# Where the first chunk's u in float32 comes from: kept from its making, or summed from its hi and lo

## The chip, the core and the metric

The kernel runs on one core of a Trainium2 chip, in one launch. The metric is the device time of one execution in microseconds (us). The core has five engines that run their own queues of instructions in the order in which they were put there and wait for one another by semaphores: PE (TensorE, products and transposes), DVE (VectorE), ACT (ScalarE), POOL (GpSimd) and SP (SyncE, which here only issues DMAs; POOL issues some too).

## The reference

What is computed is two layers of a diffusion backbone on 512 latent tokens and 256 context tokens of width 1024. Each layer is a half-step SwiGLU, a token mixer and a second half-step SwiGLU; the mixer of the first layer is an RG-LRU beside windowed attention, that of the second is dense attention. Each of the six sub-layers has the form below.

```python
def _rmsnorm(x, g):
    return x * lax.rsqrt(jnp.mean(x * x, axis=-1, keepdims=True) + EPS) * g

def _modulate(h, shift, scale):
    return h * (1 + scale) + shift

def _ffn_sublayer(h, shift, scale, gate, g_pre, g_post, w_gate, w_up, w_down):
    u = _modulate(_rmsnorm(h, g_pre), shift, scale)
    y = (jax.nn.silu(u @ w_gate) * (u @ w_up)) @ w_down
    return h + FFN_RES * gate * _rmsnorm(y, g_post)
```

## The kernel before

All six sub-layers run on one core, one after the other. Products are made in float32 from float32r passes: an operand is split exactly into hi (its 12 leading bits, a cast on ACT) and lo (the rest, a subtraction on DVE; both are issued by `halves`, L193, or by `hilo`, L724 and L725), and hi\*hi, hi\*lo and lo\*hi are summed. The 768 tokens are six tiles of 128, in two chunks of three tiles (512 tokens in two chunks of two tiles in the last two sub-layers, where the context is no longer wanted).

**The end of a sub-layer.** Its last product is token-major and is made by `type2`, once for each chunk: the down projection of a SwiGLU (names such as `d010a` and `d011a`: layer 0, second SwiGLU, chunk 0 and chunk 1) or the out-projection of a mixer (`eo0a`, `eo1a` of the first layer's, `oo0a`, `oo1a` of the second's). `type2` steps over k-tiles of 128 rows of the weights. For each it loads and splits the weights (`d011w`, 1024 columns as two halves) and makes the left operand: `hr` is a load of 128x384, `hh` its hi and lo; in the out-projections `oh` and `ooh` are made from tiles that lie in SBUF. With three token tiles a k-tile takes 18 matmuls of 512 columns (three tiles, two halves, three passes), with two token tiles 12. The last four k-tiles (`STAG`) are taken tile by tile, and each token tile then goes to `finish`.

**The boundary.** `boundary` squares and weighs the sum y of a token tile (L505, L506) and returns `rest`, which loads the residual x (L512, on POOL's queue), updates it (L514, DVE), stores it (L518) and calls `make_u`. `make_u` normalises x (the square with its sum on ACT, L410; the scaling on POOL, L414), transposes it in eight blocks on PE (`b_0utp`, L419), applies shift and scale (four blocks on ACT, L395; four on DVE, L393) into `ut`, a tile of float32 from the two slots of the tag `bu`, and splits `ut` into hi and lo, columns of the next u (L193, `u_0h`, `u_0l`).

**Where it stands.** For the tiles of the first chunk, `rest` is not run at once: it is put on the list `later`, and the `type2` of the second chunk takes one entry from `later` at each odd k, before the weights and the left operand of that k. The boundary of the first chunk's three tiles thus lies beside the second chunk's products.

**The sums.** A SwiGLU takes its features from the third on by seven block products instead of eight, for which sums of blocks of u are wanted, T1 to T4. An object of the class `Sums` makes them ahead of three sub-layers: the second SwiGLU of layer 0 and both SwiGLUs of layer 1. It needs the first chunk's u in float32. `Sums.prepare` makes it anew: hi plus lo, in six or four tiles of 128x512, two for each token tile, by POOL (L437), 16 instructions in all. `prepare` is the last entry of `later`. The three places are the second chunks of the products ahead of them, `eo1`, `d011` and `oo1`; the SwiGLU at the very start has a class of its own (`FirstSums`).

**Slots and order.** The tiles of `prepare` come from the tag `c3`, which has 23 slots of 3 KB a partition; `hr`, `hh`, `oh` and `ooh` take slots of the same tag. A scheduler places the instructions on the engines by a model of when each could run, and what is placed decides the order on the chip; slots of a tag are handed out in the order in which the program asks for them, so a tile is not begun before the tiles asked for ahead of it on its tag have their slots.

Of the kernel before, what the change touches and what calls it, by code (L numbers as in the profile page):

```python
"""Two-layer diffusion backbone (SwiGLU halves around an RG-LRU / windowed-attention mixer and a
dense-attention mixer) on one core.

float32 products run as float32r passes: an operand is split exactly into hi (its 12 leading bits)
and lo (the rest), and hi*hi + hi*lo + lo*hi is accumulated in float32.
"""
# [6 lines left out]
F32 = mybir.dt.float32  # L13
# [4 lines left out]
P = 128  # L18
# [10 lines left out]
class Net:  # L29
# [5 lines left out]
    # ---------------------------------------------------------------- set-up  # L35
# [17 lines left out]
    def psum_phase(self, all=False):  # L53
        """Six banks, or all, change hands: what follows waits bank by bank for what came before."""
        while len(self.pools) > (0 if all else 1):
            self.pools.pop().__exit__(None, None, None)
        self.nph = getattr(self, "nph", 0) + 1
        self.accs = 4 if all else 3
        self.pp = self.psum_pool(f"psum{self.nph}")
# [17 lines left out]
    def c3(self, shape, dt, name):  # L77
        """A tile of at most 3 KB a partition, from the slots that h and the mixers share."""
        return self.sb.tile(shape, dt, tag="c3", bufs=23, name=name)

    def late(self, ins):
        """A load that keeps its place behind what was issued before it on its queue."""
        return self.tc.keep_in_program_order(ins)
# [7 lines left out]
    # ------------------------------------------------- adaLN modulation, blocks 2p and 2p+1 of 18  # L91
    def tick(self, n=1):
        """n steps of the work that runs beside the rest."""
# [10 lines left out]
    def ada_steps(self, p):  # L104
        nc, cp = self.nc, self.cp
        acc = self.adatile(f"ada{p}")
        for k in range(KD):
            raws = []
            for b in range(2):
                l, j = divmod(2 * p + b, 9)  # L110
                src, name = self.a["w_ada"][l, k * P:(k + 1) * P, j * D:(j + 1) * D], f"wa{p}_{k}{b}"
                if p > 2:
                    # room where nothing else is now
# [57 lines left out]
    # ------------------------------------------------------------- weights  # L171
# [5 lines left out]
    def weights(self, src, name):  # L177
        """A [128, n] block of weights as hi and lo, 512 columns at a time."""
# [12 lines left out]
    def halves(self, hi, lo, src, eng=None, late=False):  # L191
        """src = hi + lo, exactly."""
# [11 lines left out]
    # ------------------------------------------------------------ residual stream and u  # L204
# [14 lines left out]
    # ------------------------------------------------- the first sub-layer's lead  # L219
    def opening(self, u, w, products):  # L220
        """The first modulation comes by halves of D, the second half's weights behind all else that the first half's
        products take: three of the four products of the first features start on the first half of D."""
# [3 lines left out]
        def ada_load(h, k):  # L226
            """Columns of half h of shift and scale."""
# [47 lines left out]
        def ada(h, ks=range(KD)):  # L275
            """The sums over even and odd tiles of D apart, so that four products run at a time."""
# [42 lines left out]
        def modulate(c, h):  # L319
            """zt -> u in float32, in place, and its hi and lo."""  # L320
# [54 lines left out]
    def make_u(self, x, z, t, i_shift, u, c, j, sums, name):  # L375
        """x [128 tokens, D] in SBUF -> columns 128j.. of u[c] (hi and lo of [128, KD, tokens]); z: room for x
        normalised. sums: also what the seven products of the next sub-layer take from u."""
# [7 lines left out]
        ut = bp.tile([P, KD, P], F32, tag="bu", bufs=2, name=name + "ut")  # L385
        ut = [ut[:, 0:4], ut[:, 4:8]]
# [11 lines left out]
        if sums is not None:  # L398
            # the tile before: what the next products wait for goes first
            sums.catch_up()  # L400
            if c == 1:
                sums.due = (j, ut, z)
# [19 lines left out]
    class Sums:  # L422
        """T1 = B12 - B11, T2 = B22 - T1, T3 = B12 - B22, T4 = B21 - T2, where u is [[B11, B12], [B21, B22]]:
        halves of D by chunks of tokens."""
# [4 lines left out]

        def prepare(self):  # L430
            """The first chunk once more in float32."""
            nc = self.net.nc
            for j in range(self.n // P):
                self.first[j] = [self.net.c3([P, 4, P], F32, f"b{h}{j}_{self.nm}") for h in range(2)]
                for h in range(2):
                    hi, lo = (x[:, 4 * h:4 * h + 4, j * P:(j + 1) * P].bitcast(F32) for x in self.u[0])
                    nc.gpsimd.tensor_add(self.first[j][h], hi, lo)  # L437
# [6 lines left out]
        def add(self, j, ut, z):  # L444
            """The columns of token tile j of the second chunk."""
# [10 lines left out]
        def most(self):  # L456
            """hi and lo of T1, T2 and T3."""
# [8 lines left out]
        def last(self):  # L466
            """T4 takes the place of B12."""
# [3 lines left out]
    class FirstSums:  # L471
        """The same from the first sub-layer's u in float32, in pairs of tiles of D."""
# [21 lines left out]
    def boundary(self, t, y, g, xsrc, xdst, nxt, name):  # L494
        """x += G * rms(y) for the tokens of tile t; then the next sub-layer's u. Frees y; the rest is returned."""
# [6 lines left out]
        for i in range(2):  # L502
            # a bank of y each
# [19 lines left out]
    # ------------------------------------------------------------ SwiGLU  # L523
# [3 lines left out]
    def ffn(self, l, s, u, sums, tiles, gate, finish, hook=None, joint=False):  # L527
        """tiles: the token tiles of the two chunks; finish(chunk, j, acc, G) takes the products."""
# [7 lines left out]
        def products(f, c, ks=range(KD)):  # L536
# [8 lines left out]
            # tiles of D first where they come one by one  # L545
# [13 lines left out]
        else:  # L559
            w[0] = self.ffn_weights(l, s, 0)  # L560
            self.rest()
            # the first features: the first chunk leads, since the second chunk's u comes late
# [10 lines left out]
        # as many tokens at a time as there are banks for  # L573
# [14 lines left out]
    def strassen(self, l, s, u, sums, n, hd, joint):  # L588
        """The features from the third on, two tiles at a time, by seven products (Strassen's, in Winograd's form):
        A = W^T in blocks of (feature tile) x (half of D), B = u in blocks of (half of D) x (chunk of tokens)."""  # L590
# [15 lines left out]
        def job(p, b, h):  # L606
# [5 lines left out]
            # the sums take the places of their terms  # L612
# [6 lines left out]
            # the banks that the features before hold longest come last  # L619
# [45 lines left out]
    def type2(self, nm, nk, lhs, nt, wsrc, finish, n=D, hook=None):  # L665
        """Token-major products: nt tiles of [128 tokens, n]; wsrc(k) is the rows of k-tile k."""
# [15 lines left out]
        for j in range(nt):  # L682
            # the very last tile by halves, so that what follows starts early
# [5 lines left out]
    def rest(self):  # L689
        """What the second chunk's tiles of the sub-layer before have left to do."""  # L690
# [13 lines left out]
    def type1(self, nm, src, nf, u, finish):  # L704
        """Feature-major products: nf tiles of [128 features, 2 chunks of tokens]; src(f) is the weights of tile f."""
# [22 lines left out]
    # ------------------------------------------------------------ RG-LRU || windowed attention  # L728
# [18 lines left out]
    def even(self, u, gate_i, finish):  # L747
# [3 lines left out]
        # recurrent branch: projection and convolution  # L751
# [88 lines left out]
        # gate of the recurrent branch  # L840
# [17 lines left out]
        # queries, keys, values  # L858
# [4 lines left out]
        def roped(src, t, name):  # L863
            """src [128 tokens, 10 heads * 64] in PSUM -> SBUF, rotated for the tokens of x."""
# [51 lines left out]
        def gelu():  # L916
            # once the tables of the recurrence are done with
# [8 lines left out]
        def qkv_early(t, acc):  # L926
            # the scores of the first tile start before the last queries are ready
# [19 lines left out]
        # attention  # L947
# [12 lines left out]
    def softplus8(self, src):  # L960
        """-8 softplus(-lam) and 8 softplus(-lam), [128, 8]."""
# [7 lines left out]
        # log1p(e) = 2 artanh(e / (2 + e))  # L969
# [15 lines left out]
    def pt(self, tp):  # L985
        """hi and lo of a block of transposed probabilities, in one of three places."""
# [436 lines left out]
```

## Time and profile before

| | |
|---|---|
| median of 3 runs | 2635.53 us |
| the three runs | 2635.57, 2626.84, 2635.53 us |
| span of the profiled execution | 2636.3 us |
| PE busy | 2546.2 us, 97% of the span |
| DVE busy | 1757.5 us, 67% |
| ACT busy | 1351.8 us, 51% |
| POOL busy | 325.3 us, 12% |

The span is that of one execution taken with the profiler; it is 0.8 us above the median of the runs. PE's share is near the whole span, but its idle time is not spread evenly: it lies at the start and at the boundaries between sub-layers, and there the chain of small steps on ACT, DVE and POOL is what a reader has to follow. PEclk in a row is the clock that TensorE was granted, 1.00 for 2.4 GHz and 0.50 for 1.2 GHz.

### The profile page before, as it was taken

The page shows a single profiled execution, that of the slowest core. Times are in us where ns is not written, and L with a number is a line of the kernel's source. Part 1 is how long each engine was busy: PE and PEld are TensorE (multiplying, and loading weights), DVE is VectorE, ACT ScalarE, POOL GpSimd, SP SyncE. Part 2 cuts the span into 40 slices and gives each one's busy share as a digit, 9 for nine tenths or more (in the row PEclk, how much of TensorE's full clock was granted, in tenths as well). Part 3 has the DMA queues.
Part 4 walks back from the last instruction along what each step waited for, and adds up shares of the span by engine and source line. Part 5 has one row for each costly group of instructions (what it writes and reads, how often), then busy time and mean ns, then how long its engine had stood idle before and what let it go on. Part 6 is the DMA issues. An engine that isn't in the chain of part 4 may idle for free.

```text
span 2636.3 us, 38740 instructions
## 1 busy us (share of the span) xinstructions
PE 2546.2 (97%) x13980; PEld 2237.5 (85%) x13980; DVE 1757.5 (67%) x3199; ACT 1351.8 (51%) x2783; POOL 325.3 (12%) x356
## 2 busy tenths in 40 slices
PE   7999999999999999999999999999999899899998
PEld 5899998889855789999888899998887667799986
DVE  5766664658777686767555767665557657899843
ACT  4444444547566654444454544444545556666632
POOL 4000000213022240000011300000122221400000
PEclk8999999999999999999999999999999999999999
DMA  7445436541387443232555332235554552544542
GB/s 275 144 160 168 152 127 206 192 160 53 119 293 266 157 141 96 96 105 100 187 184 189 124 97 95 98 107 177 198 181 152 200 176 82 177 135 128 161 167 88
DMA packets 147761, 403.00 MB, mean 153 GB/s; under 512 B 16504, under 2 KB 33576, under 8 KB 147568
## 3 DMA queue, kind: packets, MB, share of 16 engines
q1 hardware_dynamic: 136688, 362.00, 41.6%
q0 software_dynamic: 10880, 38.53, 4.2%
q8 instruction: 109, 1.79, 0.3%
q14 instruction: 84, 0.69, 0.1%
HBM read 351.91 MB, written 48.55 MB: 152 GB/s over the span
## 4 chain that ended last, share of the span: by engine, by line
PE 80%; DVE 7%; issue 5%; ACT 3%; POOL 3%; DMA 2%; POOLq 0%; DVEq 0%; ACTq 0%; SPq 0%
PE px L601 17%; PE py L601 12%; PE pz L601 12%; PE d110a L701 4%; PE d100a L701 4%; PE d000a L701 4%; PE d010a L701 4%; PE ada L122 3%; PE d001a L701 3%; PE d101a L701 3%; PE eo0a L701 1%; PE oq1a L701 1%; PE qkv1a L701 1%; PE opT L1286 1%; PE gu L201 1%
## 5 line engine op out<-in xcount | busy, mean ns | idle before, releaser
L210 POOL TENSOR_TENSOR b_0pr<-b_0pv,mhalf 128x1 f32<-128x1 f32 x4 | 2.2, 560 | 983.9 <-DVE b_0pv L208 983.9
L634 DVE TENSOR_TENSOR cp<-px,cp 128x384 f32<-128x384 f32 (+1 forms) x160 | 76.5, 520 | 56.3 <-PE px L601 56.3
L724 ACT ACTIVATE hh<-hr 128x384 fp32r<-128x384 f32 x132 | 68.6, 521 | 81.5 <-DMA hr<-hd 80.6
L725 DVE TENSOR_TENSOR hh<-hr,hh 128x384 fp32r<-128x384 f32 x132 | 72.9, 559 | 50.6 <-ACT hh L724 49.5
L636 ACT ACTIVATE h<-cp 128x384 f32<-128x384 f32 (+1 forms) x160 | 77.0, 498 | 26.1 <-DVE cp L634 21.9
L122 PE MATMUL ada<-wa,sc 128*32 128x512 f32 x512 | 83.8, 611 | 0.5 <-DVE cols L137 0.4
L634 DVE TENSOR_TENSOR cp<-pz,cp 128x384 f32<-128x384 f32 (+1 forms) x80 | 41.9, 524 | 57.4 <-PE pz L601 56.4
L638 DVE TENSOR_TENSOR h<-cp,h 128x384 f32<-128x384 f32 (+1 forms) x160 | 79.6, 519 | 0.4
L629 ACT ACTIVATE cp<-px 128x384 f32<-128x384 f32 (+1 forms) x160 | 71.4, 446 | 0.0
L634 DVE TENSOR_TENSOR cp<-py,cp 128x384 f32<-128x384 f32 (+1 forms) x80 | 41.7, 521 | 26.7 <-PE py L601 17.2
L614 DVE TENSOR_TENSOR w<-w,w 128x512 f32<-128x512 f32 x80 | 56.8, 709 | 1.6 <-DMA w<-in_wgu_dram 0.2
L193 DVE TENSOR_TENSOR d110w_0lo<-d110w,d110w_0hi 128x512 fp32r<-128x512 f32 x22 | 15.2, 691 | 63.6 <-ACT d110w_0hi L193 63.6
L617 DVE TENSOR_TENSOR w<-w,w 128x512 f32<-128x512 f32 x80 | 55.3, 691 | 2.0
L615 DVE TENSOR_TENSOR w<-w 128x512 f32<-128x512 f32 x80 | 55.2, 690 | 1.9
L616 DVE TENSOR_TENSOR w<-w,w 128x512 f32<-128x512 f32 x80 | 55.1, 689 | 1.5
L701 PE MATMUL d011a<-d011w_0hi,hh 128*128 128x512 f32 x132 | 52.7, 399 | 0.2 <-ACT hh L724 0.2
L701 PE MATMUL d101a<-d101w_0hi,hh 128*128 128x512 f32 x132 | 52.5, 398 | 0.0
L701 PE MATMUL d001a<-d001w_0hi,hh 128*128 128x512 f32 x132 | 52.5, 398 | 0.0
L701 PE MATMUL d100a<-d100w_512hi,hh 128*128 128x512 f32 x132 | 52.4, 397 | 0.0
L701 PE MATMUL d000a<-d000w_512hi,hh 128*128 128x512 f32 x132 | 52.4, 397 | 0.0
L701 PE MATMUL d010a<-d010w_0hi,hh 128*128 128x512 f32 x132 | 52.3, 396 | 0.0
L701 PE MATMUL d101a<-d101w_512hi,hh 128*128 128x512 f32 x132 | 52.2, 396 | 0.0
(5579 smaller groups left out, 9579.9 us busy)
## 6 DMA issues: line engine op xcount, KB each, us to landing
w<-in_wgu_dram SPq DMA_DIRECT2D x175, 512.0 KB, 3.5
wa<-in_w_ada_dram SPq DMA_DIRECT2D x204, 256.0 KB, 4.6
hd<-h SPq DMA_DIRECT2D x66, 384.0 KB, 4.7
hr<-hd SPq DMA_DIRECT2D x132, 192.0 KB, 3.7
wa<-in_w_ada_dram SPq DMA_DIRECT2D x42, 512.0 KB, 4.3
d000w<-in_w_down_dram SPq DMA_DIRECT2D x22, 512.0 KB, 3.5
d001w<-in_w_down_dram SPq DMA_DIRECT2D x22, 512.0 KB, 3.8
d010w<-in_w_down_dram SPq DMA_DIRECT2D x22, 512.0 KB, 3.9
```

What stands on the lines that cost most here:

```text
L122: ins = nc.tensor.matmul(acc[32 * g:32 * g + 32, :], lhsT=self.sc[:, k, :], rhs=raws[g], start=(k == 0), stop=(k == KD - 1), skip_group_ch ...
L601: mm = lambda x, y, **kw: nc.tensor.matmul(out, lhsT=x, rhs=y, skip_group_check=True, **kw)
L614: nc.vector.tensor_sub(x3, x1, x3)
L615: nc.vector.tensor_add(x1, x1, x2)
L617: nc.vector.tensor_sub(x4, x4, x2)
L629: nc.scalar.activation(t, src, AF.Copy)
L634: nc.vector.tensor_add(t, acc, t)
L636: nc.scalar.activation(hc, t, AF.Silu)
L638: nc.vector.tensor_mul(hc, t, hc)
L701: mm(acc[:, h:min(h + 512, n)], lhsT=x[xi][:, js], rhs=w[h // 512][wi], start=(k == 0 and xi == 0 and wi == 0), stop=(k == nk - 1 and xi = ...
L724: self.nc.scalar.activation(t[:, 0], src, AF.Copy)
L725: self.nc.vector.tensor_sub(t[:, 1], src, t[:, 0].bitcast(F32))
```

## The change

In `make_u`, where the tile belongs to the first chunk and the next sub-layer has a `Sums`, the float32 u is no longer written into the shared tile of the tag `bu`. It goes into two tiles of 128x512 of the tag `c3`, which are entered in `sums.first` and stay there until the sums have used them. `prepare`, its 16 additions on POOL and its entry in `later` are gone. The tiles of `c3` are now asked for in `make_u`, that is at k = 1, 3 and 5 of the second chunk (1 and 3 in `oo1`), ahead of the left operand of that k. Comments are left out of the file too, so line numbers move: L701 becomes L696, L724 and L725 become L719 and L720, L395 and L393 become L399 and L397, L410 and L414 become L414 and L418, L419 becomes L423, L505 becomes L500, L514 becomes L509.

```diff
@@ make_u
-        ut = bp.tile([P, KD, P], F32, tag="bu", bufs=2, name=name + "ut")
-        ut = [ut[:, 0:4], ut[:, 4:8]]
+        if sums is not None and c == 0:
+
+            ut = sums.first[j] = [self.c3([P, 4, P], F32, f"{name}b{h}") for h in range(2)]
+        else:
+            ut = bp.tile([P, KD, P], F32, tag="bu", bufs=2, name=name + "ut")
+            ut = [ut[:, 0:4], ut[:, 4:8]]
...
@@ class Sums
-        def prepare(self):
-            """The first chunk once more in float32."""
-            nc = self.net.nc
-            for j in range(self.n // P):
-                self.first[j] = [self.net.c3([P, 4, P], F32, f"b{h}{j}_{self.nm}") for h in range(2)]
-                for h in range(2):
-                    hi, lo = (x[:, 4 * h:4 * h + 4, j * P:(j + 1) * P].bitcast(F32) for x in self.u[0])
-                    nc.gpsimd.tensor_add(self.first[j][h], hi, lo)
...
@@ body
-                if sn is not None and (c, j) == (0, len(tl[s][0]) - 1):
-                    self.later.append(sn.prepare)
```

The order of the instructions on the engines moves at the three places. In the names below `hh_1` is the left operand of k-tile 1 of `d011`, and so on; `x4` after a row stands for four instructions alike.

PE in `d011` before, where the transposes of the first token tile stand:

```order
L701 MATMUL d011a_13188<-d011w_0hi,hh_1_13269 128x512
L701 MATMUL d011a_13188<-d011w_512hi,hh_1_13269 128x512
L419 MATMUL b_0utp_13235<-ident,b_0y 128x128 x4
L419 MATMUL b_0utp_13246<-ident,b_0y 128x128 x4
L701 MATMUL d011a_13189<-d011w_0hi,hh_1_13269 128x512
L701 MATMUL d011a_13189<-d011w_512hi,hh_1_13269 128x512
```

PE in `d011` after, from the last matmuls of k-tile 0:

```order
L696 MATMUL d011a_13180<-d011w_0hi,hh_0_13193 128x512
L696 MATMUL d011a_13180<-d011w_512hi,hh_0_13193 128x512
L423 MATMUL b_0utp_13227<-ident,b_0y 128x128 x4
L423 MATMUL b_0utp_13238<-ident,b_0y 128x128 x4
L423 MATMUL b_1utp_13328<-ident,b_1y 128x128 x4
L423 MATMUL b_1utp_13339<-ident,b_1y 128x128 x4
L696 MATMUL d011a_13178<-d011w_0hi,hh_1_13261 128x512
```

Before, the 18 matmuls of k-tile 0 and 12 of k-tile 1 stand ahead of the transposes; after, k-tile 0 alone does, and the second tile's transposes follow at once.

ACT before, at the end of `d010`, ahead of the first square of the boundary:

```order
L193 ACTIVATE d010w_512hi<-d010w_13049 128x512
L724 ACTIVATE hh_5_13469<-hr_5_13467 128x384
L193 ACTIVATE d010w_0hi<-d010w_13064 128x512
L193 ACTIVATE d010w_512hi<-d010w_13064 128x512
L724 ACTIVATE hh_6_13502<-hr_6_13500 128x384
L505 ACTIVATE b_0q,b_0s<-d010a_12422 128x512 x2
```

ACT after, in `d011`, from the first tile's shift and scale:

```order
L399 ACTIVATE b_0ub_13225<-b_0utp_13227,cols_7779,gs_8146 128x128 x4
L193 ACTIVATE u_0h<-b_0ub_13225 128x4x128
L193 ACTIVATE u_0h<-b_0ub_13226 128x4x128
L719 ACTIVATE hh_1_13261<-hr_1_13259 128x384
L414 ACTIVATE b_2y,b_2uss<-b_2x 128x1024
L719 ACTIVATE hh_2_13294<-hr_2_13292 128x384
L399 ACTIVATE b_1ub_13326<-b_1utp_13328,cols_7779,gs_8146 128x128 x4
```

Before, the casts of k-tiles 0 to 6 of `d011` are done ahead of the boundary; after, that of k-tile 1 stands behind the first tile's `b_0ub`, and those of 3 and 5 behind `b_1ub` and `b_2ub` in the same way.

PE in `eo1` after, from the last matmuls of k-tile 0 (`oh_8800`) to the first of k-tile 1 (`oh_8866`):

```order
L696 MATMUL eo1a_8789<-eo1w_0hi,oh_8800 128x512
L696 MATMUL eo1a_8789<-eo1w_512hi,oh_8800 128x512
L423 MATMUL b_0utp_8834<-ident,b_0y 128x128 x4
L423 MATMUL b_0utp_8845<-ident,b_0y 128x128 x4
L423 MATMUL b_1utp_8931<-ident,b_1y 128x128
L696 MATMUL eo1a_8787<-eo1w_0hi,oh_8866 128x512
```

Here one transpose of the second tile stands ahead of k-tile 1; the rest of them, and the first four of the third tile, come after k-tile 2, ahead of k-tile 3. On POOL nothing moves but the 16 additions that are gone.

## Rows read from the trace of the kernel before

**Rows 1.** The page: the span, and busy time of each engine.

```profile
PE 2546.2 (97%) x13980; PEld 2237.5 (85%) x13980; DVE 1757.5 (67%) x3199; ACT 1351.8 (51%) x2783; POOL 325.3 (12%) x356
```

**Rows 2.** Line 437: durations in ns (min/median/max), first and last start; who waited.

```profile
L437 POOL TENSOR_TENSOR b<-u_0h,u_0l x16: 1282/1596/2876, 910.9 to 2258.8; 128x512 f32<-128x512 f32 x16
...
who waited for it (us, times):
```

**Rows 3.** Stretches: length, busy PE PEld DVE ACT POOL, PEclk, DMA share, GB/s.

```profile
899.50:926.00 26.50, 25.12 (x119) 19.87 (x118) 21.63 (x40) 18.30 (x39) 16.42 (x17) 1.00 0.68 238
1365.00:1401.00 36.00, 35.50 (x165) 28.47 (x164) 27.38 (x47) 22.30 (x46) 19.99 (x18) 1.00 0.70 235
2262.30:2265.70 3.40, 3.40 (x10) 2.61 (x9) 0.41 (x1) 0.00 (x0) 0.00 (x0) 0.50 0.60 165
```

**Rows 4.** Timeline of PE in d011: start, duration, operation, [idle before <-releaser].

```profile
1365.12 0.40 PE L701 MATMUL d011a<-d011w_0hi,hh 128*128 128x512 f32 x1
...
1368.16 0.40 PE L701 MATMUL d011a<-d011w_512hi,hh 128*128 128x512 f32 x1
...
1372.63 1.09 PE L419 MATMUL b_0utp<-ident,b_0y 128*128 128x128 f32 x8 [0.34 <-POOL b_0y L414]
```

**Rows 5.** Timeline of POOL in d011.

```profile
1374.17 1.12 POOL L414 TENSOR_SCALAR b_1y<-b_1x,b_1ur 128x1024 f32<-128x1024 f32 x1
```

**Rows 6.** Timeline of ACT in d011.

```profile
1373.32 1.50 ACT L395 ACTIVATE b_0uut<-b_0utp,cols,gs 128x128 f32<-128x128 f32 x4 [0.90 <-PE b_0utp L419]
1374.86 0.63 ACT L193 ACTIVATE u_0h<-b_0uut 128x512 fp32r<-128x512 f32 x1
...
1397.43 0.52 ACT L724 ACTIVATE hh<-hr 128x384 fp32r<-128x384 f32 x1 [2.83 <-DMA hr<-hd]
```

**Rows 7.** Timeline of DVE in d011.

```profile
1379.19 1.28 DVE L514 SCALAR_TENSOR_TENSOR b_2x<-b_2y,b_2pr,b_2x 128x1024 f32<-128x1024 f32 x1 [2.98 <-DMA b_2x<-xd]
1380.39 0.69 DVE L193 TENSOR_TENSOR u_0l<-b_0uut,u_0h 128x512 fp32r<-128x512 f32 x1
...
1381.60 1.79 DVE L193 TENSOR_TENSOR d011w_512lo<-d011w,d011w_512hi 128x512 fp32r<-128x512 f32 x1
...
1397.99 0.56 DVE L725 TENSOR_TENSOR hh<-hr,hh 128x384 fp32r<-128x384 f32 x1 [2.26 <-ACT hh L724]
```

**Rows 8.** The page: issues of the left operand's loads, KB and us to landing.

```profile
hr<-hd SPq DMA_DIRECT2D x132, 192.0 KB, 3.7
```

**Rows 9.** Timelines of PE and POOL in eo1.

```profile
899.70 0.40 PE L701 MATMUL eo1a<-eo1w_0hi,oh 128*128 128x512 f32 x1
...
907.19 1.09 PE L419 MATMUL b_0utp<-ident,b_0y 128*128 128x128 f32 x8 [0.34 <-POOL b_0y L414]
...
908.74 1.12 POOL L414 TENSOR_SCALAR b_1y<-b_1x,b_1ur 128x1024 f32<-128x1024 f32 x1
```

**Rows 10.** Timelines of PE and POOL in oo1; gu is the next sub-layer's first product.

```profile
2238.36 0.40 PE L701 MATMUL oo1a<-oo1w_0hi,ooh 128*128 128x512 f32 x1
...
2249.15 1.09 PE L419 MATMUL b_2utp<-ident,b_2y 128*128 128x128 f32 x8 [1.75 <-POOL b_2y L414]
...
2256.72 0.38 PE L200 MATMUL gu<-u_0h,w_0hi 128*128 128x256 f32 x1 [0.49 <-ACT w_0hi L193]
...
2261.49 0.50 PE L701 MATMUL oo1a<-oo1w_0hi,ooh 128*128 128x512 f32 x1 [2.50 <-DVE ooh L725]
...
2270.38 0.28 PE L202 MATMUL gu<-u_0h,w_0lo 128*128 128x256 f32 x1
...
2250.69 1.12 POOL L414 TENSOR_SCALAR b_3y<-b_3x,b_3ur 128x1024 f32<-128x1024 f32 x1
```

**Rows 11.** Timeline of DVE in oo1, just ahead of the operand ooh.

```profile
2259.36 1.74 DVE L193 TENSOR_TENSOR w_0lo<-w,w_0hi 128x512 fp32r<-128x512 f32 x1
```

**Rows 12.** Timeline of PE: two transposes behind waits, elsewhere in the run.

```profile
948.26 1.97 PE L419 MATMUL b_4utp<-ident,b_4y 128*128 128x128 f32 x8 [2.37 <-POOL b_4y L414]
...
2284.66 1.10 PE L419 MATMUL b_5utp<-ident,b_5y 128*128 128x128 f32 x8 [2.27 <-POOL b_5y L414]
```

## The prediction

> **What bounds the kernel now.** I read the busy line of the page first: PE is busy for 97% of the span and no other engine for more than 67% [rows 1]. A gain has to come out of PE's idle time, and a loss is whatever new idle time PE gets. So the first question is whether anybody waits for the work that goes. The view of line 437 says no: 16 additions of 1.3 to 2.9 us on POOL, and nothing stands under its list of those who waited [rows 2]. The second question is what PE does at the three places where the additions stood. The table of stretches shows it nearly full in two of them: 35.50 of 36.00 us in d011 and 25.12 of 26.50 us in eo1 [rows 3]. What keeps it full is that the second chunk's operands lie ready while the boundary of the first chunk runs on ACT, DVE and POOL. In oo1 the cover is thinner: one wait of 1.75 us there and one of 2.50 us [rows 10].
>
> **What goes.** 16 additions of about 1.6 us, some 26 us of POOL [rows 2], which is busy for 12% of the span [rows 1]. On the path to the end they are worth nothing by themselves. They do slow a neighbour: a subtraction of 128x512 on DVE takes 0.69 us [rows 7] alone and 1.79 us beside an addition (in d011, the same rows), and about eight of them are so long. PE waits for such a one only in oo1, at its 2.50 us [rows 10, 11].
> The Trainium skill's page "SBUF — State Buffer", section "Who interferes with whom", says that DVE and POOL share a pair of ports under an exclusive lock. The 1.79 us against 0.69 us agrees; by that rule alone the change would be a small gain, and it is the mechanism of rival B.
>
> **What the change adds.** No instruction; but the float32 tiles now come from the slots of hr, hh, oh and ooh and are asked for ahead of the left operand of k = 1, 3 and 5. They are written only after the transposes of their token tile, so the operands from k = 1 on can't be got ready during the product before. The orders show it: on PE only k-tile 0 stands ahead of the transposes, and on ACT the cast of hh_1 stands behind b_0ub. What follows is a walk down the new orders with durations of the old trace.
>
> *d011.* A k-tile is 18 matmuls at 0.234 us (13 of them lie between 1365.12 and 1368.16), 4.2 us [rows 4]. PE starts k-tile 0 at 1365.1 and ends it at 1369.3. The transposes b_0utp wait for b_0y, whose chain of steps the change leaves where it was, until 1372.6: a wait of 3.3 us. They end at 1373.7 [rows 4]. b_1utp waits for b_1y on POOL, done at 1374.17 + 1.12 = 1375.3 [rows 5]: 1.6 us. It ends at 1376.4. hh_1's cast stands on ACT behind b_0ub (to 1374.8), two casts of u_0h (to 1376.1) and takes 0.52: 1376.6 [rows 6], a wait of 0.3. PE then does the 8 matmuls that take the hi half, to 1378.5, and needs the lo half. That stands on DVE behind b_2x, which waited for a load until 1379.19, and u_0l, done at 1380.39 + 0.69 = 1381.1; with 0.56 of its own it is there at 1381.6 [rows 7]: 3.1 us. The operands of k = 2 to 4 come while PE works. Then b_2utp stands ahead of k-tile 5, and hh_5 stands on ACT behind the splits of k-tile 8 of the weights (2 x 0.6, free once k-tile 4 is done), four of b_2ub (1.5), two casts (1.1) and its own 0.5: 4.3 us, of which the transposes cover 1.1 [rows 4, 6]. 3.2 us. Together 3.3 + 1.6 + 0.3 + 3.1 + 3.2 = 11.5 us, less the 0.5 us that PE idles there now [rows 3]: **+11.0**.
>
> *eo1.* From 899.70 k-tile 0 lasts to 903.9; b_0utp comes at 907.19: 3.3 us. It ends at 908.3, and the one transpose of b_1utp waits for b_1y, done at 908.74 + 1.12 = 909.9 [rows 9]: 1.6. Two k-tiles follow (8.4 us), then eleven transposes (1.4), and k-tile 3 waits for its cast behind two splits (1.1, after k-tile 2), four of b_1ub (1.5) and 0.4 [rows 6]: 3.0 less 1.4, 1.6. Sum 6.5, less the 1.4 us of idle time that stand there now [rows 3]: **+5.1**.
>
> *oo1.* 12 matmuls from 2238.36 last to 2241.2; the transposes come at 2249.15 [rows 10], so PE idles for 8.0 us where now it takes the operands that lie ready. It ends them at 2250.2 and waits for b_3y, done at 2250.69 + 1.12 = 2251.8 [rows 10]. Two transposes and 24 matmuls (5.9) take it to 2257.7; k-tile 3 stands behind a split (0.6), b_3ub (1.5) and its cast (0.4), to 2260.2. The last 60 matmuls take 14.0, to 2274.2. Before, they were done when gu went on at 2270.38, with two matmuls of gu (about 0.25 together) already made at 2256.72 [rows 10]. The 2.50 us wait and the half-clock stretch behind it [rows 3], which would go, are in that 2270.38. So **+4.0**.
>
> *The clock.* Two waits of 2.37 and 2.50 us [rows 10, 12] were followed by slow work: eight transposes that took 1.97 instead of 1.10 us, and 3.40 us at a granted 0.50, which is the lower level, 1.2 GHz [rows 3]. A wait of 2.27 us was not [rows 12]. Such a stretch, full of matmuls, does half its work and costs 1.7 us. In d011 the two waits of 3.1 and 3.2 us are followed by dense matmuls: **+3.4**. After the first wait of each place only transposes follow, which have to wait for b_1y (b_3y) anyway, so I take nothing there; at most 1.7 each. The lower bound is nothing at all, the upper bound 5 x 1.7 = 8.5 us.
>
> *Loads.* The loads of hr from k = 1 on move behind weight loads on SP's queue, since their slots come later. hr_5 has three of them ahead, the last free when k-tile 7's weights are split, some 2 us after PE is done with k-tile 3; with 3.7 us to land [rows 8] it comes while ACT is still on b_2ub. I take zero; a landing late by its own length would cost 3.7 us once.
>
> *Sum.* 11.0 + 5.1 + 4.0 + 3.4 = 23.5 us. PE is without gaps behind each place until the next boundary, and that boundary hangs on PE's last matmuls, so I carry the sum to the end. The profiled execution of 2636.3 us becomes 2659.8. It lies 0.8 us above the median of the runs; so the forecast is **2659 us**, 0.9% slower.
>
> **The rivals.** A measurement of this kernel can tell about 0.5%, or 13 us, from no change.
>
> *A, the loss is mostly made good.* The waits that no reordering hides are those for b_0y and b_1y: 4.9 - 0.5 in d011, 4.9 - 1.4 in eo1, and the 4.0 of oo1, 12 us in all. If the casts of k = 1, 3 and 5 cost nothing beyond that, because the boundary's steps run sooner on an ACT and a DVE that no longer make hh_3 to hh_6 just ahead of them, and the clock holds, the time is 2635.5 + 12 = 2647 us: no change that can be told. For it: weight loads run ahead, and a PE that waits in one place finds shorter waits in the next. Against it: b_2x waits for a load, which nothing speeds up [rows 7].
>
> *B, the other side: faster.* Place: the end of oo1. Without additions, DVE's split takes 0.69 instead of 1.74 us [rows 11], two or three of them stand ahead of ooh, and the wait of 2.50 us goes, with its half-clock stretch of 1.7 us [rows 3, 10]: 4.2 us at most, 2631 us. It decides the sign only if the new order costs under 4 us in all three places, that is if the operands of k = 1 were ready by the time PE ends k-tile 0. The order on ACT speaks against that: hh_1 stands behind b_0ub, and b_0ub behind transposes that come 3.3 us after k-tile 0's end.
>
> *C, worse.* All five long waits bring a half-clock stretch (8.5 instead of 3.4) and one load of hr lands late (3.7): 2659 + 5.1 + 3.7 = 2668 us.
>
> *D, the change does nothing.* The 16 additions are gone from POOL's order and the three places are laid out anew, so this can't be more than A.
>
> **How the numbers follow.** The forecast (2650 to 2664) has 0.74; C (above 2664) 0.10; A (2640 to 2649) 0.12, B 0.04. For 8 in 10 the range takes in the forecast, half of A and half of C: 2645 to 2669. Slower by over 0.5% (above 2648.7) is the forecast and C, 0.84; within 0.5% is A and half of B, 0.14; faster 0.02.
>
> **What would show it.** Right: in the changed profile PE waits at its first transposes of eo1 and d011 for about 3 us each with POOL's b_0y as releaser, and of oo1 for about 8; further waits of about 3 us stand ahead of matmuls of d011, released by the lo half of hh_1 (DVE) and the cast of hh_5 (ACT); half-clock rows follow. DVE's splits there are all near 0.7 us. The lengths from the first matmul of d011 to the last are up by about 14 us. Wrong: PE's idle time in d011 stays below 5 us, or the waits stand there and the span is no longer, so that a later stretch gave the time back.

## The result, and the profile after

The changed kernel took 2656.0 us (median of 4 runs, 2654.38 to 2659.15), the kernel before beside it 2631.74 us (4 runs, 2626.84 to 2635.57). The ratio is 1.009, with a 95% interval of 1.0064 to 1.0116: slower by about 24 us, as forecast (2659, 2645 to 2669).

The page says at once where not to look. POOL's busy time is down by 29 us against [rows 1] and DVE's by 10 us, and the kernel is slower. The two lines are the page of the changed kernel: span, and busy time of each engine.

```profile
span 2655.1 us, 38716 instructions
...
PE 2548.8 (96%) x13980; PEld 2236.4 (84%) x13980; DVE 1747.9 (66%) x3199; ACT 1351.6 (51%) x2783; POOL 296.2 (11%) x340
```

What to look at are the three places, from the first matmul of the second chunk's product to the last. The next two fences are tables of stretches for eo1, d011 and oo1: length, busy time and instructions of PE, PEld, DVE, ACT, POOL, then PEclk, DMA share and GB/s. The kernel before:

```profile
899.70:940.00 40.30, 37.98 (x176) 29.83 (x175) 30.73 (x57) 26.86 (x60) 24.39 (x25) 1.00 0.55 195
1365.10:1462.90 97.80, 96.36 (x428) 77.46 (x427) 57.22 (x99) 49.98 (x102) 25.17 (x25) 1.00 0.56 185
2238.40:2270.10 31.70, 26.89 (x114) 20.69 (x113) 24.88 (x44) 19.29 (x43) 14.00 (x13) 0.95 0.64 214
```

The changed kernel:

```profile
899.10:946.40 47.30, 40.29 (x177) 31.55 (x176) 31.48 (x62) 28.75 (x65) 13.48 (x18) 0.93 0.47 167
1372.20:1486.30 114.10, 102.84 (x429) 81.79 (x428) 56.98 (x105) 52.56 (x108) 14.44 (x19) 0.94 0.50 170
2252.20:2289.00 36.80, 27.53 (x113) 21.75 (x112) 22.89 (x48) 20.83 (x47) 7.92 (x10) 0.86 0.50 171
```

The lengths grew by 7.0, 16.3 and 5.1 us, 28.4 in all, for the same matmuls but two of gu (0.38 us each), which lie in oo1 in the kernel before alone [rows 10]. The table splits that into two causes. Length less PE's busy time is idle time: 2.3, 1.4 and 4.8 us before, 7.0, 11.3 and 9.3 after, 19.0 us more. The other 9.4 us are busy time of PE that grew, by 2.3, 6.5 and 0.6 us, although no matmul was added: the granted clock, whose mean in the three places fell to 0.93, 0.94 and 0.86.

The waits are the ones that the new order has. The timeline of PE in d011 of the changed kernel, its rows with idle time ahead but for the last (0.95 us at b_3utp, 0.94 before), answers to [rows 4]:

```profile
1375.73 0.50 PE L696 MATMUL d011a<-d011w_0hi,hh 128*128 128x512 f32 x1 [0.55 <-DVE b_2y L501]
1379.59 1.09 PE L423 MATMUL b_0utp<-ident,b_0y 128*128 128x128 f32 x8 [2.20 <-POOL b_0y L418]
1382.31 1.97 PE L423 MATMUL b_1utp<-ident,b_1y 128*128 128x128 f32 x8 [1.62 <-POOL b_1y L418]
1389.47 0.80 PE L696 MATMUL d011a<-d011w_0hi,hh 128*128 128x512 f32 x1 [2.80 <-DVE hh L720]
1411.41 0.50 PE L696 MATMUL d011a<-d011w_0hi,hh 128*128 128x512 f32 x1 [3.12 <-ACT hh L719]
```

The wait of 2.80 us is for the lo half of hh_1. The timeline of DVE at that moment shows what stood ahead of it, as in [rows 7]: an update of b_2x that waits for a load, then u_0l.

```profile
1387.06 1.28 DVE L509 SCALAR_TENSOR_TENSOR b_2x<-b_2y,b_2pr,b_2x 128x1024 f32<-128x1024 f32 x1 [3.89 <-DMA b_2x<-xd]
1388.26 0.68 DVE L193 TENSOR_TENSOR u_0l<-b_0ub,u_0h 128x512 fp32r<-128x512 f32 x1
1388.87 0.55 DVE L720 TENSOR_TENSOR hh<-hr,hh 128x384 fp32r<-128x384 f32 x1
```

The wait of 3.12 us is for the cast of hh_5. The timeline of ACT has two splits that were free only when PE was done with k-tile 4, then b_2ub, two casts of u and the cast itself, 4.1 us in a row:

```profile
1407.22 0.63 ACT L193 ACTIVATE d011w_0hi<-d011w 128x512 fp32r<-128x512 f32 x1 [3.05 <-PE d011a L696]
1407.76 0.61 ACT L193 ACTIVATE d011w_512hi<-d011w 128x512 fp32r<-128x512 f32 x1
1408.28 1.49 ACT L399 ACTIVATE b_2ub<-b_2utp,cols,gs 128x128 f32<-128x128 f32 x4
1409.80 1.15 ACT L193 ACTIVATE u_0h<-b_2ub 128x512 fp32r<-128x512 f32 x2
1410.85 0.51 ACT L719 ACTIVATE hh<-hr 128x384 fp32r<-128x384 f32 x1
```

In eo1 the waits ahead of the transposes are these, in the timeline of PE:

```profile
906.51 1.12 PE L423 MATMUL b_0utp<-ident,b_0y 128*128 128x128 f32 x8 [2.20 <-POOL b_0y L418]
909.23 0.47 PE L423 MATMUL b_1utp<-ident,b_1y 128*128 128x128 f32 x1 [1.59 <-ACT oh L719]
922.72 0.63 PE L423 MATMUL b_2utp<-ident,b_2y 128*128 128x128 f32 x4 [1.72 <-ACT b_1ub L399]
```

In oo1 the long wait is that for b_2y, 6.96 us against 1.75 in [rows 10]; the timeline of PE of the changed kernel:

```profile
2262.13 1.97 PE L423 MATMUL b_2utp<-ident,b_2y 128*128 128x128 f32 x8 [6.96 <-POOL b_2y L418]
2264.89 0.66 PE L423 MATMUL b_3utp<-ident,b_3y 128*128 128x128 f32 x2 [0.79 <-POOL b_3y L418]
2275.12 0.50 PE L696 MATMUL oo1a<-oo1w_0hi,ooh 128*128 128x512 f32 x1 [1.52 <-ACT ooh L719]
```

The half-clock stretches behind these waits, in the table of stretches of the changed kernel (eo1, three in d011, oo1; PEclk is the third column from the end). The stretches are cut a little short here; in full they last 6.8, 3.4, 6.8, 3.4 and 10.2 us:

```profile
907.80:914.10 6.30, 4.87 (x12) 3.91 (x13) 4.80 (x9) 2.93 (x8) 1.88 (x3) 0.50 0.75 252
1382.00:1385.30 3.30, 2.99 (x11) 2.77 (x12) 0.78 (x2) 1.39 (x3) 0.86 (x2) 0.50 0.92 314
1389.00:1395.30 6.30, 5.83 (x14) 4.57 (x15) 3.96 (x10) 4.54 (x12) 2.46 (x4) 0.50 0.50 162
1412.70:1415.90 3.20, 3.20 (x9) 2.49 (x8) 0.52 (x1) 0.52 (x1) 0.00 (x0) 0.50 0.72 271
2262.10:2269.20 7.10, 6.28 (x20) 5.05 (x21) 3.33 (x8) 3.15 (x8) 2.90 (x4) 0.50 0.64 218
```

In these rows PE was busy for 23.2 us at 1.2 GHz, where the kernel before had the one stretch of 3.40 us of [rows 3].

One thing must be known to read spans here. The two profiles differ by 18.8 us, not 28.4. From the last matmul of d011 to the first of the next down projection the kernel before took 341.1 us (1462.9 to 1804.0) and the changed one 331.7 (1486.3 to 1818.0), for the same work in the same order. Two things in that stage differ. One is a pace; the table of stretches, 100 us in the middle of it, before and then after:

```profile
1640.00:1740.00 100.00, 100.00 (x568) 100.00 (x567) 68.75 (x115) 47.11 (x88) 0.00 (x0) 1.00 0.27 93
```

```profile
1640.00:1740.00 100.00, 100.00 (x578) 100.00 (x578) 70.51 (x119) 47.58 (x89) 0.00 (x0) 1.00 0.30 105
```

PE is full and the granted clock is 1.00 in both, but 568 matmuls went through in one and 578 in the other, 1.8% or some 5.5 us over the stage. The other is the boundary behind d011, whose last transposes (b_5utp) waited 3.25 us before and 1.06 us after; the timelines of PE, before and then after:

```profile
1481.67 1.97 PE L419 MATMUL b_5utp<-ident,b_5y 128*128 128x128 f32 x8 [3.25 <-POOL b_5y L414]
```

```profile
1504.39 1.09 PE L423 MATMUL b_5utp<-ident,b_5y 128*128 128x128 f32 x8 [1.06 <-POOL b_5y L418]
```

There is more half clock in the former as well: 6.8 us at 0.50 about b_5utp, against 3.4 us behind b_4utp in the latter. Together that makes up the 9.4 us. Neither needs the change: two profiles of one and the same kernel, at the end of this text, differ in both ways too. So I compare the lengths of the three places from profiles, which agree within 0.2 us in the kernel that was profiled twice, and medians of many runs.

### The profile page after: what moved, and what is told of

Read it like the earlier page. It is cut to its first block, busy times and chain, and to the rows that moved or that the text cites. A ratio compares the mean times of both kernels' runs of the same rounds, so it can differ in the third digit from the quotient of the medians.

```text
span 2655.1 us, 38716 instructions
## 1 busy us (share of the span) xinstructions
PE 2548.8 (96%) x13980; PEld 2236.4 (84%) x13980; DVE 1747.9 (66%) x3199; ACT 1351.6 (51%) x2783; POOL 296.2 (11%) x340
## 4 chain that ended last, share of the span: by engine, by line
PE 79%; issue 8%; DVE 6%; ACT 3%; POOL 3%; DMA 2%; POOLq 0%; DVEq 0%; ACTq 0%; SPq 0%
PE px L596 17%; PE pz L596 11%; PE py L596 11%; PE d110a L696 4%; PE d100a L696 3%; PE d010a L696 3%; PE d000a L696 3%; PE ada L122 3%; PE d101a L696 3%; PE d001a L696 3%; PE eo0a L696 1%; PE qkv1a L696 1%; PE gu L201 1%; PE gu L202 1%; PE gu L200 1%
## 5 line engine op out<-in xcount | busy, mean ns | idle before, releaser
L719 ACT ACTIVATE hh<-hr 128x384 fp32r<-128x384 f32 x132 | 68.4, 520 | 76.4 <-DMA hr<-hd 76.1
L720 DVE TENSOR_TENSOR hh<-hr,hh 128x384 fp32r<-128x384 f32 x132 | 73.0, 562 | 47.9 <-ACT hh L719 47.3
L696 PE MATMUL d011a<-d011w_0hi,hh 128*128 128x512 f32 x132 | 54.6, 415 | 6.5 <-ACT hh L719 3.1
L696 PE MATMUL d011a<-d011w_512hi,hh 128*128 128x512 f32 x132 | 54.1, 412 | 0.0
L696 PE MATMUL d001a<-d001w_0hi,hh 128*128 128x512 f32 x132 | 52.5, 398 | 0.0
L696 PE MATMUL d101a<-d101w_0hi,hh 128*128 128x512 f32 x132 | 52.5, 398 | 0.0
L696 PE MATMUL d100a<-d100w_512hi,hh 128*128 128x512 f32 x132 | 52.3, 396 | 0.0
L696 PE MATMUL d000a<-d000w_512hi,hh 128*128 128x512 f32 x132 | 52.3, 396 | 0.0
L696 PE MATMUL d010a<-d010w_512hi,hh 128*128 128x512 f32 x132 | 52.3, 396 | 0.0
```

Source lines behind the costliest of these rows:

```text
L696: mm(acc[:, h:min(h + 512, n)], lhsT=x[xi][:, js], rhs=w[h // 512][wi], start=(k == 0 and xi == 0 and wi == 0), stop=(k == nk - 1 and xi = ...
L719: self.nc.scalar.activation(t[:, 0], src, AF.Copy)
L720: self.nc.vector.tensor_sub(t[:, 1], src, t[:, 0].bitcast(F32))
```

## The experiments

The theory is that the operands come late because their slots of the tag c3 stand behind tiles that are asked for ahead of them and written late. One rival, S, is that the slots run short, since six of 23 are held longer. Another, W, is that the write into other tiles or the missing additions themselves do it. Lengths are given in the order eo1, d011, oo1; the kernel before has 40.3, 97.8, 31.7 and the changed one 47.3, 114.1, 36.8.

**The float32 tiles asked for early.** They get their slots at the end of the first chunk's product, ahead of all the operands, and a first small write that holds nobody up.

```diff
@@ make_u
-            ut = sums.first[j] = [self.c3([P, 4, P], F32, f"{name}b{h}") for h in range(2)]
+            ut = sums.first[j]
@@ boundary, ahead of rest()
+        if nxt is not None and nxt[4] is not None and nxt[2] == 0:
+            b = nxt[4].first[nxt[3]] = [self.c3([P, 4, P], F32, f"{name}b{h}") for h in range(2)]
+            for h in range(2):
+                nc.gpsimd.memset(b[h][:, 0, 0:1], 0.0)
```

> The changed kernel, but the float32 tiles are asked for one step earlier: at the end of the first chunk's product, ahead of all left operands of the second chunk, and one column of each is set to zero by POOL at once, so that the tile has its slot and nothing waits behind it. POOL's additions stay away. Lengths are from the first to the last matmul of a second chunk's product; the kernel before had 40.3 (eo1), 97.8 (d011), 31.7 (oo1) us, the changed one 47.3, 114.1, 36.8. Theory (the operands are late because their slots stand behind tiles that are written late): the lengths go back to 40 and 98, oo1 to 28 to 32, since DVE's splits are no longer beside additions; the time is that of the kernel before or up to 4 us less. Rival S (too few slots: six of 23 are held longer, so the operands find no room): d011 stays above 105 us, since here they are held longest. Rival W (it is the write into other tiles or the missing additions themselves): 47, 114, 37 as in the changed kernel.

Measured: 38.5, 97.4, 25.8 us; 2628.66 us (12 runs) against 2630.49 (29 runs) before, a ratio of 0.9973 (0.9954 to 0.9992). All of the loss is gone, with the write, the missing additions and the operands' place in the program as in the changed kernel, so W falls. The six slots are held longest here, so S falls too. The places are 8.1 us shorter than before, twice what I had expected.

**The operands asked for first.** The opposite way to the same end: k-tiles 0 to 6 ask for their slots ahead of the boundaries.

```diff
@@ type2
+        ops = [lhs(k) for k in range(7)] if self.later else []
         for k in range(nk):
...
-            e = (k, self.weights(wsrc(k), f"{nm}w{k}"), lhs(k))
+            e = (k, self.weights(wsrc(k), f"{nm}w{k}"), ops[k] if k < len(ops) else lhs(k))
```

> The changed kernel, but the left operands of k-tiles 0 to 6 of the second chunk ask for their slots before the first chunk's boundaries do; the float32 tiles follow them. Theory: 40, 98 and 28 to 32 us, time as before or up to 4 us less. Rival S (too few slots): the operands have theirs, so this recovers, and with a bad result of the run with early tiles would speak for it. Rival W: as the changed kernel.

Measured: 38.6, 97.4, 26.0 us; 2620.13 us (10 runs), a ratio of 0.9963 (0.9947 to 0.9979). The table of stretches of this kernel, for the three places, has PEclk at 1.00 throughout:

```profile
899.00:937.60 38.60, 37.31 (x177) 30.09 (x176) 28.60 (x57) 26.61 (x60) 14.96 (x19) 1.00 0.57 202
1362.70:1460.10 97.40, 96.11 (x429) 77.49 (x428) 54.00 (x99) 49.79 (x102) 14.96 (x19) 1.00 0.54 186
2223.50:2249.50 26.00, 24.20 (x113) 19.41 (x112) 20.95 (x42) 18.98 (x41) 8.82 (x10) 1.00 0.68 238
```

**The additions kept, but at once.** The kernel before, in which each token tile's additions and their tiles follow its own make_u, so that the tiles are asked for at k = 1, 3 and 5, as in the changed kernel.

```diff
@@ make_u
             sums.catch_up()
+            if c == 0:
+                sums.prepare(j)
@@ Sums
-        def prepare(self):
+        def prepare(self, j):
...
-            for j in range(self.n // P):
@@ body
-                    self.later.append(sn.prepare)
```

> The kernel before, with the float32 u made as before in the two slots of bu and POOL's 16 additions kept, but each token tile's additions and their tiles are asked for at the end of its own make_u, at k = 1, 3 and 5, instead of after all of them. Theory (place of the request): slow although the additions are back and the write is the old one, and slower than the changed kernel, since the operands now stand behind two additions of 1.5 us more each: d011 115 to 123 us, eo1 47 to 54, oo1 37 to 42. Rival W: 40, 98, 32 as before.

Measured: 51.4, 123.4, 37.2 us; 2682.45 us (2 runs), a ratio of 1.0188 (1.0152 to 1.0224). The place of the request alone makes the kernel slow, with all the work and the old write kept; behind two more additions the operands come later still, and d011 is a little over the range that I had set. In the timeline of PE in its d011 the waits are longer than in the changed kernel:

```profile
1405.54 0.69 PE L421 MATMUL b_2utp<-ident,b_2y 128*128 128x128 f32 x2 [9.52 <-POOL b_2y L416]
1432.16 0.80 PE L703 MATMUL d011a<-d011w_0hi,hh 128*128 128x512 f32 x1 [7.10 <-ACT hh L726]
```

Ahead of the cast that ends the second wait, ACT itself had waited 3.79 us for the load of hr.

**The change in d011 alone.**

```diff
-        if sums is not None and c == 0:
+        if sums is not None and c == 0 and sums.nm == "3":
```

(with `prepare` left in place for the other two).

> The change at one of the three places alone, d011; eo1 and oo1 are as before. Theory (three separate losses that add): d011 114 us, eo1 40, oo1 32; the time is 15 to 17 us above the kernel before where the pace of the rest is the same. Rival (the places feed one another, or the loss is made good later): d011 shorter by some us, or a total under 12 us.

Measured: 40.4, 111.0, 31.4 us; a median of 2647.16 us (8 runs, 2634.19 to 2657.28) against 2630.49, 16.7 us more, a ratio of 1.0061 (1.0038 to 1.0084, or 10 to 22 us). Most of the loss is the place's own, and it is carried to the end. d011 was 3.1 us shorter than in the changed kernel, which I had put down as a sign of the rival. Its long waits are the same but for one, that for hh_1's lo half, whose b_2x had its load sooner; in the timeline of PE:

```profile
1372.59 1.09 PE L422 MATMUL b_0utp<-ident,b_0y 128*128 128x128 f32 x8 [2.20 <-POOL b_0y L417]
1375.30 1.88 PE L422 MATMUL b_1utp<-ident,b_1y 128*128 128x128 f32 x8 [1.62 <-POOL b_1y L417]
1381.09 0.50 PE L704 MATMUL d011a<-d011w_0hi,hh 128*128 128x512 f32 x1 [1.24 <-DVE hh L728]
1400.28 0.80 PE L704 MATMUL d011a<-d011w_0hi,hh 128*128 128x512 f32 x1 [3.13 <-ACT hh L727]
```

1.24 us instead of 2.80 is 1.6 us of waiting. The rest is the clock: d011 has 10.2 us at 0.50 here (3.4 and 6.8) against 13.6 in the changed kernel (3.4, 6.8 and 3.4). The 6.8 us that followed the 2.80 us there are missing behind the 1.24; but the 3.13 us, the same wait as the 3.12 there, were followed by 6.8 us instead of 3.4. Whether b_2x's load came sooner because eo1 was as before was not tried.

**What the additions cost.** The kernel with the operands first, and POOL's 16 additions back at their old place, into tiles that nobody reads. The sums are made from the kept tiles.

```diff
@@ Sums
+        def again(self):
...
+                    nc.gpsimd.tensor_add(t[:, 4 * h:4 * h + 4], hi, lo)
@@ body
+                    self.later.append(sn.again)
```

> The run with the operands first (38.6, 97.4, 26.0 us in eo1, d011, oo1), with POOL's 16 additions put back where they were; their results go into the two slots of bu and nobody reads them, and the sums go on to use the tiles kept from make_u. What differs from the run with the operands first is the additions alone, from the kernel before the source of the sums alone. Theory (the 8 us that the runs with the operands in time gained on the kernel before are the additions' hold on DVE): DVE's splits beside them take 1.8 us again, and the lengths go back to 40, 98 and 31 to 32 us. Rival (the gain is the direct write or the new order): 38.6, 97.4 and 26 us stay.

Measured: 39.4, 97.3, 30.0 us; 2630.42 us (10 runs) against 2627.72 (23 runs), a ratio of 1.0015 (1.0003 to 1.0027). The theory and the rival were each half right. The additions cost 0.8, nothing and 4.0 us, nearly 5 of the 8 us by which the places with the operands in time are shorter than before. The other 3 us come with the new order; of them I can name only the two matmuls of gu and their wait of 0.49 us [rows 10], which are gone from oo1. In the medians these 3 us do not show: this kernel took 2.7 us more than the one before. Where the 4.0 us are is seen in oo1 on DVE, a split as in [rows 11], and on POOL an addition beside it; DVE's row first:

```profile
2259.95 1.76 DVE L193 TENSOR_TENSOR oo1w_512lo<-oo1w,oo1w_512hi 128x512 fp32r<-128x512 f32 x1
```

```profile
2259.51 3.33 POOL L440 TENSOR_TENSOR again<-u_0h,u_0l 128x512 f32<-128x512 f32 x2 [1.23 <-DVE u_0l L193]
```

The same split takes 0.69 us in the kernel with the operands first. The exclusive lock of DVE and POOL that the Trainium skill states ("SBUF — State Buffer", "Who interferes with whom") agrees with these rows. PE waits for it and for ooh, and slow matmuls follow; in the timeline of PE:

```profile
2261.77 0.49 PE L705 MATMUL oo1a<-oo1w_512lo,ooh 128*128 128x512 f32 x1 [1.13 <-DVE oo1w_512lo L193]
2263.18 0.50 PE L705 MATMUL oo1a<-oo1w_0hi,ooh 128*128 128x512 f32 x1 [0.92 <-DVE ooh L729]
```

**Three operands ahead instead of seven.**

```diff
-        ops = [lhs(k) for k in range(7)] if self.later else []
+        ops = [lhs(k) for k in range(3)] if self.later else []
```

> The run with the operands first, with three k-tiles ahead (0 to 2) instead of seven. Theory (PE lives on the operands that are ready, 4.2 us for each k-tile of d011 and eo1, 2.8 of oo1): the first two transposes find PE still at work and their waits go; those of the third tile now stand ahead of k-tile 3 and wait for b_2y, some 20 us after the start where PE comes at 15: one wait of 4 to 5 us and a half-clock stretch behind it. d011 102 to 105 us, eo1 42 to 45; oo1 28 to 32, whose transposes come at 10.8 us where three k-tiles last 8.4. Rival (what counts is only that k-tile 1 is ready): 97.4, 38.6 and 26 us.

Measured: 45.7, 105.7, 32.6 us; 2644.97 us (2 runs), a ratio of 1.0068 (1.0049 to 1.0087). The more operands lie ready, the smaller the loss: d011 takes 97.4 us with seven ahead, 105.7 with three, 114.1 in the changed kernel. Each length is a little over the upper end that I had set. The timeline of PE in d011 shows the wait that I had expected, somewhat shorter, and one more, for the cast of hh_3:

```profile
1391.33 1.09 PE L423 MATMUL b_2utp<-ident,b_2y 128*128 128x128 f32 x8 [3.67 <-POOL b_2y L418]
1393.90 0.79 PE L697 MATMUL d011a<-d011w_0hi,hh 128*128 128x512 f32 x1 [1.49 <-ACT hh L720]
```

That cast did not stand behind other work: ACT was idle ahead of it, for the load of hr_3, which SP issued only at 1389.37, behind two loads of weights. The timeline of ACT:

```profile
1393.33 0.52 ACT L720 ACTIVATE hh<-hr 128x384 fp32r<-128x384 f32 x1 [1.37 <-DMA hr<-hd]
```

With the two waits come 6.8 us at half clock, where I had counted one stretch of 3.4.

**The operands first, once more.**

> The run with the operands first once more, for its time. Theory: places 38.6, 97.4 and 26.0 us, 8 us in all below the kernel before, a ratio of 0.997 (0.994 to 0.999); the rest of the program is the same and differs from execution to execution by the pace of the SwiGLU stages.

Measured: 38.6, 97.4, 25.8 us, as the first time; 2626.13 us (12 runs), a ratio of 0.9988 (0.9975 to 1.0). So this version takes about 1% less than the changed kernel. Against the kernel before it was 0.37% less the first time and 0.12% the second, where the interval ends at 1.0; the places are 8 us (0.3%) shorter in both profiles, and that the whole program gains as much is not shown. The change costs nothing where the kept tiles don't hold up the operands, and may gain a little.

## Why the prediction was right, step by step

**What goes.** Right in this: nobody waited for the additions, and in the changed kernel their 26 us of POOL bought nothing that made up for the loss, though DVE's 40 splits of weights in d011 all took 0.68 to 0.69 us there, as forecast. Rival B's mechanism is real, though: with the operands in time the change gains 8 us in the three places. I had put 4.2 us on it, all in oo1, and the measured share of the additions is nearly 5 us, 4.0 of it in oo1. Its condition, operands that are ready when k-tile 0 ends, was the point that decided, and the changed kernel doesn't meet it.

**The waits.** Right in place, nearly all in releaser, and near in size. In d011 I counted 3.3, 1.6, 0.3, 3.1 and 3.2 us; measured were 2.20 (and 0.55 some 4 us ahead of it), 1.62, none, 2.80 and 3.12. With what PE idled there before, 11.0 were forecast and 9.8 came. In eo1 5.1 were forecast and 4.7 came; the second wait there is released by a cast of oh and not by b_1y, though both end at 909.2 us, and the third stands ahead of the last four transposes and not behind them. In oo1 the 8.0 us for b_2y were 6.96 and the later waits 0.79 and 1.52 instead of 1.6 and 2.5 (in the 2.5 lie six transposes, 0.7 us, which the walk left out).

**The clock.** This is the term that was mis-sized: 3.4 us, with an upper bound of 8.5. The 23.2 us of PE's work at half clock would have taken half of that at the full clock, so the stretches cost 11.6 us. (PE's busy time grew by 9.4 and not by 11.6, since the old stretch in oo1, 1.7 us, and gu's two matmuls are gone from it.) The step that failed is the sentence that after the first wait of each place only transposes follow, so that a slow clock there costs nothing. In eo1 one transpose follows the second wait and then dense matmuls, and the slow rows last 6.8 us and take in eleven of these matmuls. In d011 the first slow rows reach into k-tile 1, and the wait of 2.80 us came with 6.8 us at half clock and not 3.4. I had also taken each wait by itself and drawn a line between 2.27 and 2.37 us from [rows 12]. Neither holds. In the run with the additions back, waits of 1.13 and 0.92 us, 1.4 us apart, were followed by 3.4 us at 0.50. And the length of a wait doesn't decide: in the run with the operands first, the waits of 1.85 and 3.25 us behind d011 (b_4utp and b_5utp) were nearly those of the kernel before (1.86 and 3.25), and the 60 us behind d011 have no row below 1.00, where the kernel before has 6.8 us of them. What does decide was not tried.

**The sum.** 23.5 us were forecast and the places grew by 28.4. Two errors lie in that, of opposite sign. The walk's 20.1 us are lengths; the 4.0 of oo1 are some 6.6 us of new idle time, less 2.5 of busy time that goes. So the walk had 22.7 us of idle time, where 19.0 came, and 3.4 of clock, where 11.6 came. Medians differ by 24.3 us in the first comparison; against the 29 and 23 runs of the kernel before that stand beside the experiments, 2630.49 and 2627.72, it is 25.5 and 28.3. That the forecast came within 3 us of the time is thus in part luck. That the sum is carried to the end was right: d011 alone moved the median by 16.7 us (10 to 22), where its length grew by 13.2.

**The rivals.** A is out: the places grew by 28 us where it had 12, nothing was made good behind the places, and what looks like it in the two profiles is the pace and the boundary of one stage. The loads of C were no cause here: every wait of PE in d011 is named above, none has hr as its releaser, and ACT went on to the casts of hh_1 and hh_5 without a wait for their loads. With three operands ahead such a load did come late, for 1.49 us. C's other half, a half-clock stretch with every long wait, came in full and went further: 11.6 us where C had 8.5.

## What to carry to other kernels

When a tile of a shared tag is moved to an earlier place in the program, look at what asks for a slot behind it. If the tile is written late, everything behind it on that tag is made late too, and PE loses what it had lying ready; here that cost 28 us without one instruction added. Ask for such a tile early and touch it at once (that the touch is needed was not tried by itself), or ask for the operands first. And where new waits of PE lie close together, allow for a slow clock behind them even where each is short: here PE's busy time grew by half as much as its waits.

## What was not expected of the hardware

The seven-product stages of the SwiGLU run at one of two paces, at a granted clock of 1.00 in both: 568 or 578 to 579 matmuls of 384 columns in 100 us. A single matmul's row reads 340 or 336 ns on the mean. In all nine profiles the pace is the same wherever I read it within a stage of some 300 us, and it can differ between two stages of one execution and between two executions of one kernel. The two profiles of the kernel with the operands first show it, 100 us each of the stages behind eo1 and behind d011; the first profile:

```profile
1050.00:1150.00 100.00, 100.00 (x579) 100.00 (x578) 69.51 (x117) 48.18 (x91) 0.00 (x0) 1.00 0.27 93
1640.00:1740.00 100.00, 100.00 (x579) 100.00 (x578) 69.71 (x118) 47.25 (x88) 0.00 (x0) 1.00 0.31 106
```

The second:

```profile
1050.00:1150.00 100.00, 100.00 (x579) 100.00 (x578) 69.79 (x117) 48.44 (x91) 0.00 (x0) 1.00 0.30 98
1640.00:1740.00 100.00, 100.00 (x568) 100.00 (x567) 68.57 (x115) 46.34 (x87) 0.00 (x0) 1.00 0.28 93
```

From d011 to the next down projection the first took 332.2 us and the second 337.7. The clock behind d011 differs as well. The transposes of b_4utp had the same wait in both; in the first no slow row followed, and b_5utp then waited 3.25 us; in the second 3.4 us at half clock followed, and b_5utp waited 1.12 us. The timelines of PE, the first profile and then the second:

```profile
1467.77 1.09 PE L423 MATMUL b_4utp<-ident,b_4y 128*128 128x128 f32 x8 [1.85 <-POOL b_4y L418]
```

```profile
1471.19 1.49 PE L423 MATMUL b_4utp<-ident,b_4y 128*128 128x128 f32 x8 [1.86 <-POOL b_4y L418]
```

Such differences are the likely cause of the spread of the runs of every kernel here (2622.41 to 2641.49 us for the kernel before). In the run with the tiles asked for early the time goes with the clock: the five executions with a mean granted clock of 0.993 or 0.994 took 2617 to 2622 us, the seven with 0.990 to 0.992 2628 to 2634. In the runs of the kernel before the time does not go with the mean clock. That the pace makes up the rest is argued and not shown, since it can't be read from a plain run. What sets the pace stays open.
